# Tile addresses modulo 128 bytes, and weight sums by halves, in a one-core hybrid decoder layer

## The chip, the cores and the metric

The kernel runs on one core of a Trainium2 chip. Its time is the device time of one execution in microseconds (us); the median of several executions is given, and lower is better.

## What is computed

One decoder layer on 256 tokens of width 1024, all in float32. The input is normalised, multiplied by one wide weight matrix, and the product is cut into the operands of three gated branches:

```python
h = rms_norm(x, norm_g)
qa, ka, va, ga, ub, vb, gb, qc, gc, ma, mb, mc = split_cols(h @ w_in, IN_SPLITS)
out_a = moba_attention(rope(qa), rope(ka), va) * silu(ga)          # 6 heads of 128, causal
out_b = gmlp_spatial_gate(ub, vb, ln_g, w_spatial, b_spatial) * silu(gb)   # 6 groups of 128
out_c = memory_cross_attention(qc, rms_norm(mem), w_mem_kv) * silu(gc)     # 4 heads of 128
y = sigmoid(ma) * (out_a @ w_branch_a) + sigmoid(mb) * (out_b @ w_branch_b) + sigmoid(mc) * (out_c @ w_branch_c)
return rms_norm(x + y @ w_out, final_norm_g)
```

With 256 tokens there is one attention block, so the attention is plain causal attention over all tokens. The wide product dominates: w_in alone has 1024 x 9472 floats.

## The kernel before, in words

**Products.** Float32 operands are split into a high part (rounded to the matmul's own format, by ScalarE, ACT) and a low part (the rest, by VectorE, DVE), and a product is made of three matmuls: high by high, high by low, low by high. Activations are split once; weights are split as they arrive, 128 partitions x 1024 floats at a time. Such a piece is called a chunk. split_hi (L258) writes tile hi and split_lo (L262) writes tile lo; each has five slots (SPL = 5), so chunk c uses the slot of chunk c - 5. The splits of chunk c are issued four chunks (LEAD = 4) ahead of its matmuls.

**Kinds of chunks**, in the order that plan() writes out by hand:
- mvk (8) and tok (4): keys and values of the memory, and some columns of v and of the spatial gate (L479, L500, L506).
- fea (30): 128 output columns each, the weights being the stationary operand and the activations n the moving one: eight matmuls of 512 columns and eight of 256 (L628). q, k, ga, gc, qc and parts of ub and gb are made so.
- st (70, in 35 pairs): a Strassen-like scheme. For each of five groups g (two blocks of 512 output columns each), seven blocks i replace eight products; the weights of a block are one of four weight blocks, or sums of them. Order: 1, 2, 5, 3, 6, 7, 4. A pair is one block, its chunks the two halves: six matmuls of 512 columns each (L568), with n or s (sums of n) as stationary operand and hi or lo moving. Group 0 gives columns of va and vb, group 1 ut and gt, groups 2, 3 and 4 the three sigmoid gates (tiles sig and sigs).
- br (16): the three branch projections, with ah and al, obh and obl, och and ocl as stationary operands, twelve matmuls of 512 columns a chunk (L446 to L448, in mm3). Between them stand the last eleven blocks of st.
- out (8): the output projection, with y as stationary operand (L446 to L448 again).

**The form tiles.** The weights of the st blocks live in two tiles of 1 MB, form0 and form1. FORMS says which tile and which weight block a block i uses; the two change places with every group. Blocks 1, 2 and 3 are plain loads, issued on SP's queue (form_load, L226). Blocks 5, 7 and 4 are made by a transfer that adds to what is there, issued on POOL's queue (form_add, L229). Block 6 adds block 3's weights, which the other tile holds at that time: in groups 0, 1 and 2 (SUMS) by a DVE instruction over the whole tile (form_sum, L240), in groups 3 and 4 by an adding transfer. All of these go by whole blocks: a transfer or a sum is issued when both halves of what the tile held have been split. Each is issued at a fixed place in the order of chunks (the lists dma, ready and free at the end of the kernel):

```python
at = free[b] + (chunks[c][2] not in (5, 6, 4, 7))     # a load one chunk later than an addition
if chunks[c][2] == 6 and chunks[c][1] in SUMS:
    at = free[1 - b]
...
free[b] = c + 2 - LEAD
```

**Other weights** come by plain loads on SP's queue into three tiles raw of 1 MB (load, L208), from pair 18 to 46 in two parts.

**Side work** (attention, gates, norms, drains of PSUM) is put between the chunks by a small planner (class Units): each step has an engine, a cost, what it comes after, and a chunk by which it is due. slot() issues what fits before and after each chunk's matmuls. A step that comes after a TensorE step is due four chunks behind that one, so that the PSUM bank comes free.

**Places of the tiles.** Pools lay their tags one behind the other in the order of first use, each as long as its largest tile. Pool act has, in this order: p1, p2, mr, xr, x2 (m, later s), och, ocl, n2 (n, later y), v0 (va, later obl), vb (later obh), trig (the rotary tables, later wspb: spatial weights and their bias, 774 floats a partition), lng, ut, gt, ga (later ah), sg0, sg1, gc (later al0), ub, v1 (al1). Pool wts follows: raw, hi, lo, f0.

Of the kernel before, what the change touches and what calls it, by code (L numbers as in the profile page):

```python
# [24 lines left out]
F32 = mybir.dt.float32  # L25
# [3 lines left out]
OP = mybir.AluOpType  # L29
# [6 lines left out]
HA, GB, HC = 6, 6, 4  # L36
# [4 lines left out]
CH = 1024  # L41
PIECE = 2 * CH
# [3 lines left out]
SPAN = {"fea": 2.78, "st": 1.365}  # L46
# [35 lines left out]
PE, DVE, ACT, POOL, QUEUE = range(5)  # L82


class Units:
# [29 lines left out]

    def fits(self, u, i, pe, now):
        name, e, us, fn, after, wait, due = u
        due = min([due] + [self.pe[a] + 4 for a in after if a in self.pe])
        if pe != (e == PE) or any(a not in self.end for a in after):
            return False  # L120
        if i >= due or e is None:
            return True
        if pe:
            return self.ready(after) + self.margin <= now
        if e == QUEUE:

            return self.ready(after) <= now
        lead = 0.5 if e == POOL else max(0.3, self.room - (2.4 if e == ACT else 1.3) - self.ahead - us)
        return self.t[e] <= now + lead and self.ready(after) <= max(now, self.t[e]) + 0.3

    def slot(self, i, pe):

        now, u = self.t[PE], True
        while u:
            if pe:
                now = self.t[PE]
            u = next((u for u in self.todo if self.fits(u, i, pe, now)), None)
            if u:
                self.todo.remove(u)
                name, e, us, fn, after, wait, due = u  # L140
                if e == PE:
                    self.pe[name] = i
                at = self.ready(after)
                self.end[name] = (at if e is None else self.run(e, us, at)) + wait
                fn()
# [3 lines left out]
def tile_hybrid_layer(ctx: ExitStack, tc: tile.TileContext, mw, xT, mem, x, fin_g, ln_g, w, ws, w_sp, b_sp, rope, out):  # L149
    nc = tc.nc  # L150
# [3 lines left out]
    wts = ctx.enter_context(tc.tile_pool(name="wts", bufs=1))  # L154
# [3 lines left out]
    V = {}  # L158

    def slot_tile(name, shape, tag, dt=F32):  # L160
        V[name] = act.tile(shape, dt, name=name, tag=tag)
        return V[name]
# [17 lines left out]
        return slice(h * 128, (h + 1) * 128)  # L180


    RAW, SPL, LEAD, JT = 3, 5, 4, 2
    raw, hi, lo = {}, {}, {}
    chunks = []
# [23 lines left out]

    def load(j):  # L210
        raw_alloc(j)
        parts = 2 if 18 <= j < 47 else 1
        for i in range(parts):
            load_part(j, i * PIECE // parts, (i + 1) * PIECE // parts)

    def block(g, i):

        return bass.AP(tensor=ws.tensor, offset=ws.offset + (4 * g + i) * 128 * PIECE, ap=[[PIECE, 128], [1, PIECE]])

    def form_tile(i):  # L220
        if f"form{i}" not in V:
            V[f"form{i}"] = (wts if i == 0 else act).tile([128, PIECE], F32, name=f"form{i}", tag=("f0", "mr")[i])
        return V[f"form{i}"]

    def form_load(i, g, b):
        nc.sync.dma_start(form_tile(i), block(g, b))  # L226

    def form_add(i, g, b):
        nc.gpsimd.dma_start(form_tile(i), block(g, b), accum_op=OP.add)  # L229


    SUMS = (0, 1, 2)
    FORMS = {1: (0, 0), 5: (0, 1), 6: (0, 3), 4: (0, 2), 2: (1, 2), 7: (1, 1), 3: (1, 3)}

    def buf(g, i):
        return FORMS[i][0] ^ (g % 2)

    def form_sum(i, g, b):

        nc.vector.tensor_tensor(form_tile(i), form_tile(i), form_tile(1 - i), OP.add)  # L240
        U.run(DVE, 2.35)

    def form_step(g, i):

        if i == 6 and g in SUMS:
            return form_sum, buf(g, i), g, 3

        return (form_add if i in (5, 6, 4, 7) else form_load, buf(g, i), g, FORMS[i][1])

    def split_alloc(c):  # L250
        if "hi" not in V:
            for n in ("hi", "lo"):
                V[n] = wts.tile([128, SPL, CH], F32R, name=n, tag=n)
        hi[c], lo[c] = V["hi"][:, c % SPL, :], V["lo"][:, c % SPL, :]

# [21 lines left out]
    st = [act.tile([128, NG + 4 * XW], F32, name="st0", tag="p1"), act.tile([128, 4 * XW], F32, name="st1", tag="p2")]  # L277
# [164 lines left out]
    U = Units(4.5, AHEAD, 1.8)  # L442
# [251 lines left out]
        nc.sync.dma_start(V["lng"], rows(ln_g, BW))  # L694

    def load_wsp():
        t = slot_tile("wspb", [128, GB * 128 + GB], "trig")
        nc.sync.dma_start(t, w_sp)
        V["wsp"], V["bst"] = t[:, 0:GB * 128].rearrange("p (g t) -> p g t", g=GB), t[:, GB * 128:]

    def cut_wsp():
        for g in range(GB):
# [11 lines left out]
    for t in range(2):  # L714
        U.add(f"xsq{t}", ACT, 1.25, lambda t=t: row_squares(V["xk"][:, t, :], ssx[:, t:t + 1]), after=[f"load_x{t}"],
              due=2 + t)
# [18 lines left out]
    for i in range(KD // 2):  # L735
        U.chain(f"nx{i}", (ACT, 0.62, lambda i=i: norm_hi(i)), (DVE, 0.7, lambda i=i: norm_lo(i)),
                after=[f"nm{2 * i}", f"nm{2 * i + 1}"] + ["s11"] * (i == 3), due=(6, 6, 8, 9)[i])
    U.chain("sum", *[(DVE, 0.69, lambda i=i: sums(i)) for i in range(4)], after=["nx3"], due=[12, 13, 14, 15])
    for i in range(2):
        U.chain(f"sx{i}", (ACT, 1.05, lambda i=i: sums_hi(i)), (DVE, 1.28, lambda i=i: sums_lo(i)), after=["sum"],  # L740
                due=18 - i)
    for t in range(2):
        U.add(f"msq{t}", ACT, 1.25, lambda t=t: row_squares(V[f"mm{t}"], ssm[:, t:t + 1]),
              after=["load_mem"])
# [168 lines left out]
    for h in range(HC):  # L913
# [3 lines left out]
                after=[f"qc{h}", f"mkf{h | 1}", "sqrts"] + back("p", h))  # L917
        U.chain(f"cn{h}", (DVE, 0.2, lambda h=h: softmax_sum("c", h)), (ACT, 0.85, lambda h=h: softmax_norm("c", h)),
                after=[f"cs{h}"])
# [3 lines left out]
    for h in range(HA):  # L923
        if h % 2 == 0:
            r = h // 2
            U.add(f"rin{r}", QUEUE, 1.6, lambda r=r: rope_move(r, False), wait=8.5,
                  after=[f"{n}{i}" for i in (h, h + 1) for n in "qk"] + ["consts"] + ([f"rout{r - 2}"] if r > 1 else []))
# [5 lines left out]
                after=[f"as{h}"])  # L933
        U.chain(f"ap{h}", (PE, 0.33, lambda h=h: a_pT(h)), (ACT, 0.52, lambda h=h: a_pT_out(h)),
                after=[f"an{h}"] + back("v", HC + h))
# [3 lines left out]
    for name, n in (("gc", HC), ("ga", HA)):  # L939
        U.add(name + "s", ACT, n * 0.25, lambda name=name: nc.scalar.activation(V[name], V[name], AF.Silu),  # L940
              after=["exps"] + [f"{name}{i}" for i in range(n)])
    U.add("silu", ACT, 1.4, lambda: nc.scalar.preload_act_table(AF.Sigmoid), after=["gcs", "gas", "gts.0", "gbs2"])

    for t in range(2):
        U.chain(f"lna{t}", (DVE, 1.0, lambda t=t: ln_centre(t)), (ACT, 0.9, lambda t=t: ln_scale(t)), after=["lnr", "gmlp"],
                due=[at_br[0, 0] - 10 + t, at_br[0, 0] - 8 + t])
# [61 lines left out]
    for i in range(3):  # L1008
        hs = slice(2 * i, 2 * i + 2)
        U.add(f"ga_{i}", DVE, 0.69, lambda hs=hs: gate_unit(V["qk"][:, hs, 0, :], V["ga"][:, hs, :]),  # L1010
              after=[f"av{2 * i}", f"av{2 * i + 1}", "gas"], due=at_br[0, 0] - 6)
# [3 lines left out]
          after=[f"cs{h}" for h in range(HC)])  # L1015
    U.chain("gts", (ACT, 1.1, lambda: nc.scalar.activation(V["gt"], V["gt"], AF.Silu)),
            (DVE, 1.25, lambda: nc.vector.tensor_tensor(V["ut"], V["ut"], V["gt"], OP.mult)),
            due=[at_br[0, 0] - 4, at_br[0, 0] - 3], after=["exps", "w11_1", "w12_1", "w22_1", "p14"])
    for i in range(2):
# [6 lines left out]
        after=["mix2", "gbs2"], due=chunks.index(("fea", "gb", 5)) + 5)  # L1026
    U.add("obTa", None, 0, alloc(("obh", [128, GB, S], "vb", F32R), ("obl", [128, GB, S], "v0", F32R)),
          after=["mix0", "mix1", "mix2"])
# [113 lines left out]
        nc.sync.dma_start(out[:, t, 512:D], z[:, 512:D])  # L1142


    dma, ready, free = {}, {}, [6, 9]
    for c in range(n_br):
        if chunks[c][0] == "st" and chunks[c][3] == 0:
            b = buf(*chunks[c][1:3])
            at = free[b] + (chunks[c][2] not in (5, 6, 4, 7))
            if chunks[c][2] == 6 and chunks[c][1] in SUMS:  # L1150
                at = free[1 - b]
            dma.setdefault(at, []).append(form_step(*chunks[c][1:3]))
            ready[c // 2] = at
            free[b] = c + 2 - LEAD
    pace = lambda c: 5.0 + sum(SPAN.get(k[0], 2.73) for k in chunks[:c])
    for c, at in ready.items():
        i = chunks[2 * c][2]
        ready[c] = pace(at) + (2.5 if i == 6 and chunks[2 * c][1] in SUMS else 10.0 if i in (4, 5, 6, 7) else 6.0)
    for c in range(n_br + 4):
        now[0] = c  # L1160
        if c == n_br:
            nc.scalar.preload_act_table(AF.Sqrt)
            residual_parts()
        if c == n_br - 8:
            load_x()
        s = c + (LEAD if c > 9 else 3)
        for fn, *args in dma.pop(c, []):
            fn(*args)
        U.room = sum(SPAN.get(k[0], 2.73) for k in chunks[c:c + LEAD])
        U.slot(c, False)  # L1170
        if c in (7, 8):
            split_lo(2 * c - 6)
            U.end[f"s{2 * c - 6}"] = U.run(DVE, 1.23, U.t[ACT])
        for e in {5: (), 6: (), 7: (9,), 8: (11,), 9: (12, 13)}.get(c, (s,) if s > 3 else ()):
            if chunks[e][0] == "st":
                raw[e // 2] = form_tile(buf(*chunks[e][1:3]))
                came = ready[e // 2]
            else:
                came = {4: 24.0, 5: 25.5}.get(e // 2, 0.0)
            (split_mvk if e < KD else split)(e)  # L1180
            U.end[f"s{e}"] = U.run(DVE, 1.23, U.run(ACT, 1.05, max(U.end.get(f"c{e - SPL}", 0), came)))
        if c in (6, 7):
            split_alloc(2 * c - 4)
            split_hi(2 * c - 4)
            U.run(ACT, 1.05, (23.5, 28.0)[c - 6])
        s += c == 9
        if s % 2 == 1 and s // 2 in PLAIN:
            q = PLAIN.index(s // 2) + 2
            if 4 < q < len(PLAIN):
                load(PLAIN[q])  # L1190
            if q == 6:
                load_mem()
        kind = chunks[c][0]
        U.end[f"c{c}"] = U.run(PE, SPAN.get(kind, 2.73), U.end.get(f"s{c}", 0.0))
        if kind == "mvk":
            mm_mvk(c)
        elif kind == "tok":
            mm_tok(c)
        elif kind == "fea":
            mm_fea(c)  # L1200
        elif kind == "br":
            mm_br(c)
        elif kind == "st":
            mm_st(c)
        else:
            mm_out(c, 0)
            for a, b in (((0, 256), (256, 512)) if chunks[c][1] else ((0, 512),)):
                mm_out(c, 1, a, b)
        U.slot(c, True)
# [115 lines left out]
```

## Time and profile before

| | |
|---|---|
| median of 3 runs | 329.92 us (329.75 to 330.6) |
| the profiled execution: its own time, and its span | 333.19 us, 331.5 us |
| busy: TensorE, DVE, ACT, POOL | 317.0, 255.5, 226.8, 25.0 us |
| mean granted TensorE clock | 0.979 |
| moved by DMA | 77.24 MB, mean 233 GB/s |
| adding transfers into the form tiles (POOL's queue) | 17 of 1 MB, 9.7 us from issue to landing |
| loads into the form tiles (SP's queue) | 15 of 1 MB, 5.0 us |

The span runs from the first to the last instruction. PE is TensorE's matmuls, PEld its loads of the stationary operand. A row of a view names the line of the kernel, the engine, the operation, and the tiles as "written<-read"; acc and aux are PSUM banks. "x" counts instructions, "<-" behind an idle time names what ended it. The granted clock is the share of TensorE's full clock.

### The profile page before, as it was taken

What the parts mean: (1) busy time and instruction counts of PE and PEld (TensorE: products, weight loads), DVE (VectorE), ACT (ScalarE), POOL (GpSimd) and SP (SyncE); (2) the same over time, 40 slices, a digit from 0 to 9 for tenths busy, and PEclk for the clock granted to TensorE, in tenths of its full rate; (3) what the DMA queues carried; (4) which work ended last, traced back from release to release, by engine and by line L of the source; (5) the groups of instructions that cost most, each with busy time, mean ns of one, the idle gap of its engine ahead of it and who ended that gap; (6) DMA issues with size and microseconds to landing.
All of it is one profiled execution on the core that took longest, in us unless ns stands there. A gap on an engine that the chain in (4) does not pass through costs nothing. (4 is left out here: it accounts for less than half of the span.)

```text
span 331.5 us, 4343 instructions
## 1 busy us (share of the span) xinstructions
PE 317.0 (96%) x1542; PEld 261.6 (79%) x1542; DVE 255.5 (77%) x369; ACT 226.8 (68%) x357; POOL 25.0 (8%) x42
## 2 busy tenths in 40 slices
PE   7999999999999999999999999989999897999992
PEld 3888888888888888888888888867887675878882
DVE  2889989977698986975986999846982939889532
ACT  3877979547977869779957967819672744487333
POOL 1000030020010011022011010111010111000022
PEclk9999999999999999999999999997999797999997
DMA  7999998669669489869659789898799697943003
GB/s 205 407 401 417 406 284 288 228 150 190 245 217 259 156 257 213 280 223 222 207 190 173 225 334 211 253 265 165 264 312 292 173 266 133 378 175 128 2 0 127
DMA packets 16294, 77.24 MB, mean 233 GB/s; under 512 B 2064, under 2 KB 3088, under 8 KB 9744
## 3 DMA queue, kind: packets, MB, share of 16 engines
q1 hardware_dynamic: 13680, 59.00, 48.3%
q0 software_dynamic: 2448, 17.83, 28.4%
q8 instruction: 12, 0.20, 0.2%
q10 hardware_dynamic: 144, 0.13, 0.1%
q14 instruction: 10, 0.08, 0.1%
HBM read 75.12 MB, written 1.05 MB: 230 GB/s over the span
## 5 line engine op out<-in xcount | busy, mean ns | idle before, releaser
L262 DVE TENSOR_TENSOR lo<-form,hi 128x1024 fp32r<-128x1024 f32 x70 | 84.1, 1219 | 35.9 <-ACT hi L258 35.5
L258 ACT ACTIVATE hi<-form 128x1024 fp32r<-128x1024 f32 x70 | 72.2, 1056 | 44.8 <-DMA form<-in_ws_dram 33.3
L262 DVE TENSOR_TENSOR lo<-raw,hi 128x1024 fp32r<-128x1024 f32 x58 | 70.0, 1221 | 12.6 <-ACT hi L258 12.2
L258 ACT ACTIVATE hi<-raw 128x1024 fp32r<-128x1024 f32 x58 | 60.8, 1058 | 14.1 <-PE acc L448 4.7
L628 PE MATMUL acc<-n,hi 128*128 128x512 f32 x240 | 61.3, 397 | 0.0
L628 PEld LDWEIGHTS acc<-n,hi 128*128 128x128 f32 x240 | 43.7, 188 | 9.0
L229 POOL DMA_DIRECT2D form<-in_ws_dram x17 | 14.9, 876 | 255.4 <-DVE lo L262 151.0
L568 PE MATMUL acc<-hi,s 128*128 128x512 f32 x96 | 33.1, 403 | 0.0
L628 PEld LDWEIGHTS acc<-n,lo 128*128 128x128 f32 x240 | 30.9, 188 | 1.5
L628 PE MATMUL acc<-n,lo 128*128 128x256 f32 x240 | 31.9, 283 | 0.0
L568 PE MATMUL aux<-hi,s 128*128 128x512 f32 x64 | 24.0, 440 | 2.5 <-ACT hi L258 2.5
L568 PE MATMUL acc<-hi,n 128*128 128x512 f32 x72 | 25.3, 408 | 0.0
L568 PEld LDWEIGHTS acc<-hi,s 128*128 128x128 f32 x96 | 18.0, 188 | 4.2
L568 PE MATMUL acc<-lo,s 128*128 128x512 f32 x48 | 18.9, 394 | 0.0
L568 PEld LDWEIGHTS aux<-hi,s 128*128 128x128 f32 x64 | 13.5, 211 | 6.5 <-ACT hi L258 3.3
L568 PE MATMUL aux<-lo,s 128*128 128x512 f32 x32 | 14.6, 457 | 3.9 <-DVE lo L262 3.9
L568 PE MATMUL aux<-hi,n 128*128 128x512 f32 x48 | 15.9, 395 | 0.0
L568 PEld LDWEIGHTS acc<-hi,n 128*128 128x128 f32 x72 | 13.5, 188 | 3.0
L568 PE MATMUL acc<-lo,n 128*128 128x512 f32 x36 | 14.2, 394 | 0.0
L568 PEld LDWEIGHTS aux<-lo,s 128*128 128x128 f32 x32 | 6.6, 206 | 6.9 <-DVE lo L262 5.5
L568 PEld LDWEIGHTS aux<-hi,n 128*128 128x128 f32 x48 | 9.0, 187 | 2.2
L568 PEld LDWEIGHTS acc<-lo,s 128*128 128x128 f32 x48 | 9.0, 188 | 1.9
(233 smaller groups left out, 578.9 us busy)
## 6 DMA issues: line engine op xcount, KB each, us to landing
raw<-in_w_dram SPq DMA_DIRECT2D x18, 1024.0 KB, 8.7
form<-in_ws_dram POOLq DMA_DIRECT2D x17, 1024.0 KB, 9.7
form<-in_ws_dram SPq DMA_DIRECT2D x15, 1024.0 KB, 5.0
raw<-in_w_dram SPq DMA_DIRECT2D x22, 512.0 KB, 7.2
st<-in_mw_dram SPq DMA_DIRECT2D x7, 384.0 KB, 7.5
raw<-in_w_dram SPq DMA_DIRECT2D x8, 256.0 KB, 7.3
xk<-in_x_dram SPq DMA_DIRECT2D x2, 512.0 KB, 7.5
xt<-in_xT_dram SPq DMA_DIRECT2D x2, 512.0 KB, 8.6
```

Source lines behind the costliest of these rows:

```text
L229: nc.gpsimd.dma_start(form_tile(i), block(g, b), accum_op=OP.add)
L258: nc.scalar.activation(hi[c][:, a:b], raw[c // 2][:, o + a:o + b], AF.Copy)
L262: nc.vector.tensor_tensor(lo[c][:, a:b], raw[c // 2][:, o + a:o + b], hi[c][:, a:b].bitcast(F32), OP.subtract)
L568: nc.tensor.matmul(p, x[:, k0 + k, tsl(t)], wt[c][:, a * 512:(a + 1) * 512], start=first and a + j == 0, stop=half == 1 and a + j == 3, sk ...
L628: nc.tensor.matmul(o, wt, m, start=i == 0, stop=i == len(passes) - 1, skip_group_check=True)
```

## The change

1. The tile wspb is 800 floats wide instead of 774; what is read and written in it stays. A pad LOPAD between hi and lo is added, of size 0.
2. Transfers and sums of the form tiles go by halves: 128 x 1024 floats, 512 KB. Each half has its own place in the order, by its own half's split.
3. Block 6 is a sum on DVE in all five groups.
4. In the planner, a step of ACT that comes after a TensorE step passes on that step's place, so that steps behind it are due four chunks later too; TensorE's own steps no longer take a due place from this.
5. Raw loads go in two parts up to pair 48 instead of 46.

```diff
     def fits(self, u, i, pe, now):
         name, e, us, fn, after, wait, due = u
-        due = min([due] + [self.pe[a] + 4 for a in after if a in self.pe])
+        due = due if pe else min([due] + [int(self.pe[a]) + 4 for a in after if a in self.pe])
...
+                up = [self.pe[a] for a in after if a in self.pe and self.pe[a] % 1 == 0]
                 if e == PE:
                     self.pe[name] = i
+                elif up and e == ACT:
+                    self.pe[name] = up[0] + 0.5
...
+    LOPAD = 0
...
-        parts = 2 if 18 <= j < 47 else 1
+        parts = 2 if 18 <= j < 49 else 1
...
-    def block(g, i):
-        return bass.AP(tensor=ws.tensor, offset=ws.offset + (4 * g + i) * 128 * PIECE, ap=[[PIECE, 128], [1, PIECE]])
+    def block(g, i, h):
+        return bass.AP(tensor=ws.tensor, offset=ws.offset + (4 * g + i) * 128 * PIECE + h * CH, ap=[[PIECE, 128], [1, CH]])
...
-    def form_load(i, g, b):
-        nc.sync.dma_start(form_tile(i), block(g, b))
-    def form_add(i, g, b):
-        nc.gpsimd.dma_start(form_tile(i), block(g, b), accum_op=OP.add)
-    SUMS = (0, 1, 2)
+    def form_half(i, h):
+        return form_tile(i)[:, h * CH:(h + 1) * CH]
+    def form_load(i, g, b, h):
+        nc.sync.dma_start(form_half(i, h), block(g, b, h))
+    def form_add(i, g, b, h):
+        nc.gpsimd.dma_start(form_half(i, h), block(g, b, h), accum_op=OP.add)
+    def form_sum(i, g, b, h):
+        nc.vector.tensor_tensor(form_half(i, h), form_half(i, h), form_half(1 - i, h), OP.add)
+        U.run(DVE, 1.23)
     FORMS = {1: (0, 0), 5: (0, 1), 6: (0, 3), 4: (0, 2), 2: (1, 2), 7: (1, 1), 3: (1, 3)}
...
-    def form_sum(i, g, b):
-        nc.vector.tensor_tensor(form_tile(i), form_tile(i), form_tile(1 - i), OP.add)
-        U.run(DVE, 2.35)
-    def form_step(g, i):
-        if i == 6 and g in SUMS:
-            return form_sum, buf(g, i), g, 3
-        return (form_add if i in (5, 6, 4, 7) else form_load, buf(g, i), g, FORMS[i][1])
+    HOW = {5: (form_add, 8.0), 7: (form_add, 8.0), 4: (form_add, 8.0), 6: (form_sum, 1.5)}
...
-        t = slot_tile("wspb", [128, GB * 128 + GB], "trig")
-        nc.sync.dma_start(t, w_sp)
+        t = slot_tile("wspb", [128, GB * 128 + 32], "trig")
+        nc.sync.dma_start(t[:, 0:GB * 128 + GB], w_sp)
...
-    dma, ready, free = {}, {}, [6, 9]
+    dma, ready, free = {}, {}, [[6, 6], [9, 9]]
+    pace = lambda c: 5.0 + sum(SPAN.get(k[0], 2.73) for k in chunks[:c])
     for c in range(n_br):
-        if chunks[c][0] == "st" and chunks[c][3] == 0:
-            b = buf(*chunks[c][1:3])
-            at = free[b] + (chunks[c][2] not in (5, 6, 4, 7))
-            if chunks[c][2] == 6 and chunks[c][1] in SUMS:
-                at = free[1 - b]
-            dma.setdefault(at, []).append(form_step(*chunks[c][1:3]))
-            ready[c // 2] = at
-            free[b] = c + 2 - LEAD
...
+        if chunks[c][0] == "st":
+            _, g, i, h = chunks[c]
+            b = buf(g, i)
+            fn, us = HOW.get(i, (form_load, 5.0))
+            at = free[1 - b][h] if i == 6 else free[b][h] + (i not in HOW)
+            dma.setdefault(at, []).append((fn, b, g, FORMS[i][1], h))
+            ready[c] = pace(at) + us
+            free[b][h] = c + 1 - LEAD
```

ready[c] is the planner's own estimate of when a piece has landed; it goes into the order of the side work alone.

More of the change, by code (lines that the diff above doesn't have):

```diff
@@ L236, in buf @@
         return FORMS[i][0] ^ (g % 2)
-    def form_sum(i, g, b):
-        nc.vector.tensor_tensor(form_tile(i), form_tile(i), form_tile(1 - i), OP.add)
-        U.run(DVE, 2.35)
-    def form_step(g, i):
-        if i == 6 and g in SUMS:
-            return form_sum, buf(g, i), g, 3
-        return (form_add if i in (5, 6, 4, 7) else form_load, buf(g, i), g, FORMS[i][1])
+    HOW = {5: (form_add, 8.0), 7: (form_add, 8.0), 4: (form_add, 8.0), 6: (form_sum, 1.5)}
     def split_alloc(c):
         if "hi" not in V:
-            for n in ("hi", "lo"):
+            for n, pad in (("hi", 0), ("lo", LOPAD)):
+                if pad:
+                    wts.tile([128, pad], F32, name=n + "pad", tag=n + "pad")
                 V[n] = wts.tile([128, SPL, CH], F32R, name=n, tag=n)
@@ L696, in load_wsp @@
     def load_wsp():
-        t = slot_tile("wspb", [128, GB * 128 + GB], "trig")
-        nc.sync.dma_start(t, w_sp)
-        V["wsp"], V["bst"] = t[:, 0:GB * 128].rearrange("p (g t) -> p g t", g=GB), t[:, GB * 128:]
+        t = slot_tile("wspb", [128, GB * 128 + 32], "trig")
+        nc.sync.dma_start(t[:, 0:GB * 128 + GB], w_sp)
+        V["wsp"], V["bst"] = t[:, 0:GB * 128].rearrange("p (g t) -> p g t", g=GB), t[:, GB * 128:GB * 128 + GB]
     def cut_wsp():
@@ L1142, in out_store @@
         nc.sync.dma_start(out[:, t, 512:D], z[:, 512:D])
-    dma, ready, free = {}, {}, [6, 9]
+    dma, ready, free = {}, {}, [[6, 6], [9, 9]]
+    pace = lambda c: 5.0 + sum(SPAN.get(k[0], 2.73) for k in chunks[:c])
     for c in range(n_br):
-        if chunks[c][0] == "st" and chunks[c][3] == 0:
-            b = buf(*chunks[c][1:3])
-            at = free[b] + (chunks[c][2] not in (5, 6, 4, 7))
-            if chunks[c][2] == 6 and chunks[c][1] in SUMS:
-                at = free[1 - b]
-            dma.setdefault(at, []).append(form_step(*chunks[c][1:3]))
-            ready[c // 2] = at
-            free[b] = c + 2 - LEAD
[L1155 to L1158, printed above, removed]
+        if chunks[c][0] == "st":
[6 more added lines that the diff above has]
+            free[b][h] = c + 1 - LEAD
     for c in range(n_br + 4):
@@ L1176, in tile_hybrid_layer @@
                 raw[e // 2] = form_tile(buf(*chunks[e][1:3]))
-                came = ready[e // 2]
+                came = ready[e]
             else:
```

## The prediction

> **What bounds the kernel now.** I read the page first, for the busy shares and the clock. "q1" is the queue of SP's transfers, "q0" that of POOL's adding ones.
>
> ```profile
> span 331.5 us, 4343 instructions
> PE 317.0 (96%) x1542; PEld 261.6 (79%) x1542; DVE 255.5 (77%) x369; ACT 226.8 (68%) x357; POOL 25.0 (8%) x42
> ...
> PEclk9999999999999999999999999997999797999997
> ...
> q1 hardware_dynamic: 13680, 59.00, 48.3%
> q0 software_dynamic: 2448, 17.83, 28.4%
> ```
>
> TensorE is busy for 96% of the span, so only two things shorten this kernel: matmuls that follow each other faster, and the few places where PE stands or runs at a lower clock. The clock row shows such places in slices 27 to 33 (8.3 us each). The table by stretches sizes them.
>
> ```profile
> 220.00:240.00 20.00, 17.72 (x70) 13.74 (x69) 14.02 (x14) 15.10 (x17) 0.86 (x1) 0.91 0.83 218
> 240.00:260.00 20.00, 18.31 (x77) 14.28 (x76) 11.85 (x13) 11.69 (x14) 0.86 (x1) 0.99 0.95 302
> 260.00:280.00 20.00, 17.57 (x62) 13.34 (x61) 14.11 (x15) 10.18 (x12) 2.60 (x3) 0.84 0.81 174
> ```
>
> Columns: length, busy PE, PEld, DVE, ACT, POOL, granted clock, DMA share, GB/s. PE stands for 2.28 + 1.69 + 2.43 = 6.4 us, and the clock takes 1.8 + 0.2 + 3.2 = 5.2 us more (20 us times what is missing to 1.00): 11.6 us in this stage. The waits from 220 to 280 us and ACT's rows say what ends them.
>
> ```profile
> POOL form L229 <- DVE lo L262: 53.5, 5, 17.2
> ACT hi L258 <- DMA form<-in_ws_dram: 24.5, 5, 7.8
> DVE lo L262 <- ACT hi L258: 21.3, 7, 6.1
> ...
> PE aux L568 <- DVE lo L262: 3.9, 4, 2.1
> PE aux L568 <- ACT hi L258: 2.5, 2, 1.5
> ```
>
> ```profile
> 222.16 2.01 ACT L258 ACTIVATE hi<-form 128x1024 fp32r<-128x1024 f32 x2 [7.77 <-DMA form<-in_ws_dram]
> ...
> 256.44 2.00 ACT L258 ACTIVATE hi<-form 128x1024 fp32r<-128x1024 f32 x2 [5.95 <-DMA form<-in_ws_dram]
> ...
> 269.76 2.01 ACT L258 ACTIVATE hi<-form 128x1024 fp32r<-128x1024 f32 x2 [5.94 <-DMA form<-in_ws_dram]
> ```
>
> Read upwards: PE waits for a split, DVE's half of it for ACT's, and ACT for an adding transfer into a form tile. By order of chunks the three are block 6 of group 3, block 5 of group 4 and block 6 of group 4. Before this stage PE is never without work; there only the rate of the matmuls counts:
>
> ```profile
> 40.00:220.00 180.00, 180.00 (x938) 152.90 (x937) 150.72 (x226) 135.14 (x228) 15.59 (x24) 1.00 0.81 232
> ```
>
> **The rate of the matmuls.** Here the trace has an experiment of its own. These stretches hold 24 matmuls of 512 columns each: two branch chunks with ah and al as stationary operand, two with obh and obl, and four of the Strassen chunks.
>
> ```profile
> 237.02:242.47 5.45, 5.45 (x25) 4.50 (x24) 5.12 (x7) 2.01 (x2) 0.00 (x0) 1.00 0.98 406
> 248.07:253.67 5.60, 5.60 (x25) 4.50 (x24) 2.36 (x2) 2.42 (x4) 0.00 (x0) 1.00 1.02 233
> 207.72:213.32 5.60, 5.60 (x26) 4.50 (x24) 5.21 (x7) 5.60 (x9) 0.86 (x1) 1.00 0.86 281
> ```
>
> 5.45/24 = 227 ns against 5.60/24 = 233 ns, at the same clock; neither DVE's nor the DMA engines' load goes with it (406 GB/s in the faster one). What goes with it is the place of the tiles. Between x2 (m, s), n2 (n, y), v0, vb, och, ocl and the tiles behind "trig" (ga/ah, gc/al0, v1/al1, hi, lo), all sizes are multiples of 128 bytes but one: wspb has 774 floats, 3096 = 24 x 128 + 24. So ah, al, hi and lo begin at one byte modulo 128, and n, s, y, obh and och at another. With 800 floats, 3200 = 25 x 128, all of these agree.
>
> **The change, part by part.**
> 1. *Alignment.* Pairs that now differ: 420 matmuls at L568 (70 half chunks by 6), 240 at L628, 120 of the branches (16 chunks by 12, less ah's 72) and 72 with y: 852 of 512 columns, by 6.2 ns: 5.3 us. Of 256 columns 240 at L628 and 48 with y; no pair of that width is aligned in this trace, so I take half, 3.1 ns, between 0 and 6.2: 0.9 us. Sum **6.2 us**. The chunks before 40 us gain nothing in my sum: the DMA share is 0.96 there, in the table by stretches.
>
> ```profile
> 0.00:40.00 40.00, 37.76 (x173) 29.38 (x174) 30.95 (x57) 29.43 (x51) 1.09 (x9) 1.00 0.96 365
> ```
>
> Bounds: whether a pair is fast because it agrees, or because both begin at a multiple of 128, the trace can't show directly, as after the change the common byte is hi's present one plus the 96 (or 104) bytes that the longer wspb pushes it. If the second, the gain is nothing, ah's 72 lose 0.4 us, and if each operand off its place costs its own 6.2 ns, 6.2 us are lost. For agreement speaks this pair of rows: the Strassen chunks have the shifted tile as stationary operand, the feature chunks as the moving one, and both take the same.
>
> ```profile
> L568 PE MATMUL acc<-hi,n x72: 389/396/587, 45.4 to 198.2; 128*128 128x512 f32 x72
> ...
> L628 PE MATMUL acc<-n,hi x240: 392/395/578, 39.8 to 207.5; 128*128 128x512 f32 x120
> ...
> L447 PE MATMUL acc<-lo,ah x24: 387/389/397, 213.6 to 242.0; 128*128 128x512 f32 x24
> ```
>
> (ns min/median/max of one.) [...] So I take 6.2, nearest to the row of ah.
>
> 2. *Block 6 by DVE in groups 3 and 4 too.* Two adding transfers of 1 MB go. The sum needs only block 3, which landed for the chunk before. The rows of the sums and of the splits:
>
> ```profile
> L240 DVE TENSOR_TENSOR form<-form,form 128x2048 f32<-128x2048 f32 x3 | 6.9, 2285 | 0.0
> L262 DVE TENSOR_TENSOR lo<-form,hi 128x1024 fp32r<-128x1024 f32 x70 | 84.1, 1219 | 35.9 <-ACT hi L258 35.5
> ```
>
> A half costs what a split does: 10 x 1.22 instead of 3 x 2.29 = +5.3 us on DVE, of it 4.9 in the late stage. There the waits at 222 and 270 us lose their cause. Cover: DVE has 65.5 us of work from 209 to 298.
>
> ```profile
> 209.00:298.00 89.00, 82.60 (x331) 64.75 (x330) 65.49 (x72) 52.76 (x59) 6.05 (x7) 0.94 0.85 241
> ```
>
> 65.5 + 4.9 = 70.4 us, while PE would need 89 - 11.6 - 1.6 (alignment) = 75.8: DVE fits at 93%. What is queued behind a sum on DVE is the next chunk's lo, 1.22 us later than without it.
>
> 3. *Halves.* Each half's transfer starts when its own half is split, instead of after both, and is half as long.
>
> ```profile
> raw<-in_w_dram SPq DMA_DIRECT2D x18, 1024.0 KB, 8.7
> form<-in_ws_dram POOLq DMA_DIRECT2D x17, 1024.0 KB, 9.7
> ...
> raw<-in_w_dram SPq DMA_DIRECT2D x22, 512.0 KB, 7.2
> ```
>
> ```profile
> 240.11 1.23 DVE L262 TENSOR_TENSOR lo<-form,hi 128x1024 fp32r<-128x1024 f32 x1 [0.34 <-ACT hi L258]
> ...
> 242.45 1.21 DVE L262 TENSOR_TENSOR lo<-form,hi 128x1024 fp32r<-128x1024 f32 x1
> ```
>
> ```profile
> 244.02 0.86 POOL L229 DMA_DIRECT2D form<-in_ws_dram  x1 [17.18 <-DVE lo L262]
> ```
>
> For block 5 of group 4 the first half may start at 241.3 (240.11 + 1.23) instead of 244.0. A half lands after 4.9 us (half of 9.7) to 9.7 us (size saves nothing); I take 7.2, the row of 512 KB. The whole came at 256.44, 12.4 us after its issue; with halves I put the first near 249 to 251 and the second near 253. PE came to that chunk behind the first of these rows, at 256.5:
>
> ```profile
> 256.24 0.39 PE L568 MATMUL aux<-hi,n 128*128 128x512 f32 x1
> 257.55 0.50 PE L568 MATMUL aux<-hi,s 128*128 128x512 f32 x1 [0.93 <-ACT hi L258]
> ```
>
> So this wait goes too, by some 3 us; at 9.7 from both issues it goes but for the second half's tail. Added issues: 15 on SP and 13 x 0.86 us on POOL, whose queues wait in this stage (53.5 us above); POOL holds nothing else then, and SP's loads wait for the same splits as before. Of 17.83 MB added by transfers, 2 MB go.
>
> Of the 11.6 us I count **10.0**: the rest for waits that come up in its place, as DVE has little left. Bounds 0 to 11.6.
>
> 4. *The order of side work.* DVE steps behind an ACT step that drains a PSUM bank are now due four chunks after the matmul: ga, gc and the obT halves, 0.7 us each, move up. Nothing is added; an early one can hold the next lo by 0.7 us once or twice, or free it later: 0, bounds +-1.4. One more raw load goes in two parts (0.4 us of SP). The pad LOPAD is 0 and does nothing.
>
> **Sum.** 333.19 us is the profiled execution's own time (span 331.5 and 1.7 around it), 1% over the median of the runs, 329.92. 333.2 - 6.2 - 10.0 = 317.0, by 329.92/333.19: **313.9 us**.
>
> [...]
>
> **Rivals.**
> A. *Alignment does nothing.* For it: no pair at the new common byte is in the trace. Against: the equal rows of L568 and L628. 333.2 - 10.0 = 323.2, that is 320.0; with 6.2 lost instead, 326.2.
> B. *The late stage keeps its loss.* DVE at 93%, in order, with sums ahead of the splits, becomes what PE waits for, and the clock drops again. For it: DVE's share; against: ACT's 24.5 us of waits go, which held DVE for 21.3. 333.2 - 6.2 = 327.0, that is 323.8.
> C. *Slower: an adding packet costs by the packet, not by its bytes.* q0's 28.4% are 94 us of all engines for 17 transfers, 615 ns a packet against 187 in q1. If halves cost as much each, 30 take 166 us, 72 more; with 0.83 of the first 302 us used (251 us), that is 323 us of transfers ahead of the output stage's 29.5: 352, that is 349. It makes the kernel slower from 302 - 157 = 145 us for q0 (157 is the rest), 0.87 of a whole one's cost for a half. Against: q1's packets have 0.6 of q0's bytes and 0.3 of its time.
>
> ```profile
> 0.00:302.00 302.00, 293.37 (x1412) 241.44 (x1413) 241.23 (x345) 215.33 (x333) 21.01 (x38) 0.98 0.83 252
> 302.00:331.50 29.50, 23.66 (x131) 20.12 (x129) 14.24 (x25) 11.50 (x25) 4.00 (x4) 0.94 0.12 43
> ```
>
> **How the numbers follow.** The forecast has 0.6, A 0.15, B 0.16, C 0.04, and a mishap that just cancels the gain 0.05. The forecast's own range is 309 (both parts in full: 7.0 with the first chunks, and 11.6, with a little of part 4) to 318. The range for 8 in 10 takes in A and B: 308 to 324.5. Within 0.3% (1 us) is about what a measurement of this kernel can't tell from no change. Faster: forecast, A and B, 0.91; same 0.04; slower 0.05.
>
> **What would show it.** Part 1: 24 matmuls of a Strassen or obh stretch in 5.45 us, and the median of one at 389; at 396 rival A. Part 2: no wait of PE at blocks 6, L240's successor 10 times at 1.22 us, and a clock row without the dips at 27 to 33. Part 3: adds of 512 KB landing near 7 us, and the 24.5 us of ACT's waits down to a few. Wrong if PE's waits are back behind DVE (B), if adds take 9 us each (C), or if a new wait shows between 40 and 220 us, where faster matmuls have less cover.

## The result, and the profile after

The changed kernel takes 320.72 us (median of 4 runs, 319.87 to 321.17) against 329.84 us (329.46 to 330.60) for the kernel before on the same chip: a ratio of 0.9718, 95% interval 0.9690 to 0.9746, or 9.1 us less. The profiled execution of the changed kernel took 320.98 us.

These are the lines of its page that answer to those shown of before: the span, the busy times, the clock row, the two queues, the splits on DVE and ACT, DVE's sums, and the issues (count, KB each, us to landing).

```profile
span 319.2 us, 4440 instructions
PE 312.0 (98%) x1542; PEld 260.1 (81%) x1542; DVE 260.2 (81%) x376; ACT 227.8 (71%) x357; POOL 36.5 (11%) x55
...
PEclk9999999999999999999999999999999999999998
...
q1 hardware_dynamic: 15984, 59.00, 52.3%
q0 software_dynamic: 4320, 15.73, 26.8%
...
L264 DVE TENSOR_TENSOR lo<-form,hi 128x1024 fp32r<-128x1024 f32 x70 | 84.8, 1222 | 16.2 <-ACT hi L260 15.7
L260 ACT ACTIVATE hi<-form 128x1024 fp32r<-128x1024 f32 x70 | 73.4, 1057 | 23.3 <-DMA form<-in_ws_dram 8.6
...
L240 DVE TENSOR_TENSOR form<-form,form 128x1024 f32<-128x1024 f32 x10 | 12.2, 1222 | 0.0
...
form<-in_ws_dram POOLq DMA_DIRECT2D x30, 512.0 KB, 8.5
raw<-in_w_dram SPq DMA_DIRECT2D x24, 512.0 KB, 7.3
```

The dips of the clock at slices 27 to 33 are gone, ACT waits 8.6 us for form tiles where it waited 24.5 in the late stage alone, and PE is busy for 98% of the span. Stretch by stretch (columns as before), with one stretch of four Strassen chunks and one of two branch chunks with obh and obl, 24 matmuls each:

```profile
40.00:220.00 180.00, 180.00 (x938) 153.31 (x937) 156.11 (x234) 141.41 (x235) 24.48 (x35) 1.00 0.84 232
220.00:240.00 20.00, 20.00 (x88) 16.35 (x87) 17.88 (x19) 13.72 (x16) 3.47 (x4) 1.00 1.02 268
240.00:260.00 20.00, 20.00 (x87) 16.21 (x87) 13.71 (x13) 12.94 (x15) 0.86 (x1) 1.00 0.83 266
260.00:280.00 20.00, 19.66 (x85) 15.61 (x84) 19.07 (x22) 12.42 (x13) 2.59 (x3) 1.00 0.97 264
```

```profile
207.61:213.18 5.57, 5.57 (x25) 4.52 (x24) 4.96 (x7) 4.93 (x6) 0.00 (x0) 1.00 0.72 249
243.54:249.11 5.57, 5.57 (x26) 4.52 (x24) 3.58 (x3) 3.37 (x5) 0.00 (x0) 1.00 0.97 268
```

Two readings. The late stage has lost its waits: PE stands for 0.34 us there, not 6.4, and the clock takes nothing. But the matmuls hardly got faster: 5.57/24 = 232 ns, against 233 before and the 227 that was forecast (the median of one at L570 is 393, between the 389 and the 396 that the prediction named as signs). And between 40 and 220 us there are 938 matmuls in both traces. The four-chunk stretch begins at 207.72 us in the trace before and at 207.61 here. The whole gain lies behind it.

### The profile page after: what moved, and what is told of

Read it like the earlier page. It is cut to its first block, busy times and chain, and to the rows that moved or that the text cites. A ratio compares the mean times of both kernels' runs of the same rounds, so it can differ in the third digit from the quotient of the medians.

```text
span 319.2 us, 4440 instructions
## 1 busy us (share of the span) xinstructions
PE 312.0 (98%) x1542; PEld 260.1 (81%) x1542; DVE 260.2 (81%) x376; ACT 227.8 (71%) x357; POOL 36.5 (11%) x55
## 3 DMA queue, kind: packets, MB, share of 16 engines
q0 software_dynamic: 4320, 15.73, 26.8%
## 4 chain that ended last, share of the span: by engine, by line
PE 77%; DMA 9%; DVE 6%; issue 4%; ACT 1%; POOL 0%; SPq 0%; ACTq 0%; POOLq 0%; DVEq 0%
PE acc L630 26%; PE acc L570 18%; DMA form<-in_ws_dram 7%; PE aux L502 3%; PE acc L508 3%; PE aux L570 3%; DVE lo L264 3%; PE acc L450 3%; PE acc L448 3%; PE acc L449 3%; PE aux L781 2%; DMA st<-in_mw_dram 2%; PE aux L481 2%; PE acc L481 2%; DVE form L240 1%
## 5 line engine op out<-in xcount | busy, mean ns | idle before, releaser
L264 DVE TENSOR_TENSOR lo<-form,hi 128x1024 fp32r<-128x1024 f32 x70 | 84.8, 1222 | 16.2 <-ACT hi L260 15.7
L260 ACT ACTIVATE hi<-form 128x1024 fp32r<-128x1024 f32 x70 | 73.4, 1057 | 23.3 <-DMA form<-in_ws_dram 8.6
L236 POOL DMA_DIRECT2D form<-in_ws_dram x30 | 26.1, 871 | 232.9 <-DVE lo L264 84.6
L570 PE MATMUL acc<-hi,s 128*128 128x512 f32 x96 | 33.1, 402 | 0.0
L570 PE MATMUL acc<-hi,n 128*128 128x512 f32 x72 | 25.1, 404 | 0.0
L570 PEld LDWEIGHTS acc<-hi,s 128*128 128x128 f32 x96 | 18.1, 188 | 4.0
L570 PE MATMUL aux<-hi,s 128*128 128x512 f32 x64 | 21.1, 395 | 0.0
L570 PE MATMUL acc<-lo,s 128*128 128x512 f32 x48 | 18.9, 395 | 0.0
L570 PE MATMUL aux<-hi,n 128*128 128x512 f32 x48 | 16.1, 396 | 0.0
L570 PEld LDWEIGHTS acc<-hi,n 128*128 128x128 f32 x72 | 13.6, 188 | 2.9
L570 PEld LDWEIGHTS aux<-hi,s 128*128 128x128 f32 x64 | 12.1, 188 | 2.8
L570 PE MATMUL acc<-lo,n 128*128 128x512 f32 x36 | 14.2, 394 | 0.0
L570 PE MATMUL aux<-lo,s 128*128 128x512 f32 x32 | 12.7, 398 | 0.3 <-DVE lo L264 0.3
L643 ACT ACTIVATE qk<-acc 128x256 f32<-128x256 f32 x12 | 4.7, 390 | 11.7 <-PE acc L630 11.7
L240 DVE TENSOR_TENSOR form<-form,form 128x1024 f32<-128x1024 f32 x10 | 12.2, 1222 | 0.0
L570 PEld LDWEIGHTS aux<-hi,n 128*128 128x128 f32 x48 | 9.0, 188 | 2.1
```

The costliest lines, as they stand in the source:

```text
L236: nc.gpsimd.dma_start(form_half(i, h), block(g, b, h), accum_op=OP.add)
L240: nc.vector.tensor_tensor(form_half(i, h), form_half(i, h), form_half(1 - i, h), OP.add)
L260: nc.scalar.activation(hi[c][:, a:b], raw[c // 2][:, o + a:o + b], AF.Copy)
L264: nc.vector.tensor_tensor(lo[c][:, a:b], raw[c // 2][:, o + a:o + b], hi[c][:, a:b].bitcast(F32), OP.subtract)
L570: nc.tensor.matmul(p, x[:, k0 + k, tsl(t)], wt[c][:, a * 512:(a + 1) * 512], start=first and a + j == 0, stop=half == 1 and a + j == 3, sk ...
```

## The experiments

In each comparison the ratio is to the kernel before, run on the same chip. Two questions were open: why the matmuls kept their rate, and which part gave the 9.1 us.

### What the rate of the matmuls goes by

wspb's length decides where hi, lo, ah and al begin against n, s, y, obh and och. It is 3096 bytes before, and 3200 = 12.5 x 256 in the changed kernel. In the kernel before, hi, lo, ah and al begin at byte 128 modulo 256, the others at 96. The longer tile brings the four to 224: they agree with the rest modulo 128, and miss them by 128 modulo 256. ah and hi agree with each other in any case. So the fast pair (hi, ah) of the trace before could mean modulo 256 or 512 (theories M256 and M512), or a matter of the region of the memory in which ah and al lie (theory R).

**Agreement modulo 512.** `[128, GB * 128 + 32]` becomes `[128, 896]` (3584 = 7 x 512 bytes).

> The changed kernel with wspb 896 floats wide instead of 800, so that hi, lo, ah and al move by 384 bytes more and every tile read by TensorE (m, s, n, y, och, obh, ah, hi, lo) begins at byte 96 modulo 512. In the changed kernel hi, lo and ah begin at 224 modulo 512 and the others at 96, and only the pairs with ah run at 227 ns, the others at 232. Theory M (agreement counts, but modulo 256 or 512 bytes and not 128): stretches of 24 matmuls in 5.45 us instead of 5.57, 852 x 5 ns = 4.3 us, and 256-column matmuls from 119 to about 114 ns, 288 x 5 = 1.4 us: 315 to 316.5 us. Theory R (what counts is that both operands lie in the upper part of SBUF, as with ah): no change, 320.7 us within 1 us, matmul medians 393 and 389 as before.

Measured: 317.93 us (6 runs), ratio 0.9635 (0.9587 to 0.9683). Behind the first 40 us the 512-column matmuls follow each other at 226 to 227 ns (medians, from one start to the next) in every pair of tiles. The rate is theory M's; its time, 315 to 316.5 us, is missed, as it had put 1.4 us on 256-column matmuls that did not speed up.

**Agreement modulo 256 only.** The same line with `[128, 832]` (3328 = 13 x 256 bytes).

> The same with wspb 832 floats wide: hi, lo, ah and al at byte 352 modulo 512, the others at 96, so that they agree modulo 256 and not modulo 512. Theory M with modulus 256: as the run with 896 floats, 315 to 316.5 us. Theory M with modulus 512: ah's pairs alone at 389 ns, the others at 393 to 396, 320.7 us within 1. Theory R: the same as that, 320.7 us.

Measured: 317.17 us (4 runs), ratio 0.9620 (0.9580 to 0.9661). The same two stretches, and the line of the Strassen chunks, in this variant:

```profile
205.37:210.81 5.44, 5.44 (x25) 4.50 (x24) 5.44 (x8) 4.93 (x6) 0.00 (x0) 1.00 0.75 264
240.73:246.17 5.44, 5.44 (x25) 4.50 (x24) 3.59 (x3) 3.45 (x5) 0.00 (x0) 1.00 1.02 331
```

```profile
L570 PE MATMUL acc<-hi,n x72: 387/389/590, 44.9 to 196.0; 128*128 128x512 f32 x72
```

5.44/24 = 227 ns: the fast rate, with agreement modulo 256 and not modulo 512. M512 and R fall. It is also the fastest kernel of the study, 3.5 us under the changed one. The 852 matmuls of 512 columns at 5 ns would make 4.3 us. The 256-column ones give a little of it back (119 ns became 120 here; 117 in the kernel before).

**lo alone moved by 128 bytes.** In the changed kernel `LOPAD = 0` becomes `LOPAD = 32`: lo now agrees with n, s and obh modulo 256 and no longer with ah, hi stays.

> The changed kernel with LOPAD at 32 floats, which moves lo alone by 128 bytes. Theory M: the pairs of lo with ah lose their agreement, and the median of acc<-lo,ah goes from 389 to 393 ns or more while hi's pairs may stay; time within 1 us of 320.7. Theory R: ah's three rows stay at 389 ns.

Measured: 322.17 us (one run). The rates part within one execution; the branch chunks' matmuls (ns min/median/max of one):

```profile
L448 PE MATMUL acc<-hi,ah x24: 397/397/398, 212.7 to 237.0; 128*128 128x512 f32 x24
L449 PE MATMUL acc<-lo,ah x24: 395/395/395, 212.9 to 237.3; 128*128 128x512 f32 x24
L449 PE MATMUL acc<-lo,obh x24: 388/388/396, 243.5 to 273.3; 128*128 128x512 f32 x24
```

Of one tile, lo, the pair with obh is now the fast one and that with ah the slow one, where the changed kernel has it the other way round (392 and 389). So it is not the tile alone that sets the rate. Nor is it the pair alone: hi and ah begin at the same byte modulo 256 as before, yet their matmuls, each followed by one of lo with ah, went from 389 to 397, which is 236 ns from one start to the next. The time, 1.5 us over the changed kernel's, is more than the 1 us that was expected, on a single run.

**No alignment at all.** The changed kernel with wspb at its old 774 floats.

> The changed kernel with the alignment alone undone: wspb 774 floats wide again, all else as changed (halves, block 6 on VectorE in all groups, planner). The forecast's step 1 (6.2 us from alignment) expects 326 to 327 us. The reading of the two traces (512-column matmuls from 234 to 232 ns, 256-column ones from 117 to 119) expects 320.7 to 321.7 us.

Measured: 320.58 us (6 runs), ratio 0.9732 (0.9698 to 0.9765), against 320.72 with it. Agreement modulo 128 is worth nothing.

**Agreement modulo 256 alone, on the kernel before.** wspb of 832 floats, nothing else changed.

> The kernel before with wspb of 832 floats alone: the stationary and moving tiles agree modulo 256, all else as before. Theory U (rate of the matmuls is independent of the rest): 512-column matmuls at 227 ns in place of 233, and the 3.5 us that the same edit gave the changed kernel: 326 to 327. Theory L (what PE gains it loses again standing for the same transfers in the late stage, which come no sooner): 328.5 to 330, with the median of L568 at 389 all the same.

Measured: 326.23 us (6 runs), ratio 0.9892 (0.9854 to 0.9929): 3.6 us less, what it gave the changed kernel. Theory U holds in its time, L in one stage. Against the second execution of the kernel before (below), PE is 3.1 us ahead at the four-chunk stretch (204.92 against 208.00) and 3.2 us at the last branch chunk (291.31 against 294.48): what the first 208 us gain is kept, and what the matmuls of the late stage gain goes into its waits, which are still there (PE stands for 6.8 us from 215 to 285 us, against 5.8 in that execution).

**lo off by 32 bytes.** The variant with 832 floats and `LOPAD = 8`.

> The variant whose tiles agree modulo 256 (317.17), with lo alone moved by 32 bytes: hi, ah, al and n, s, y, och, obh still agree, lo differs from them by 32. Asked: do the 256-column matmuls (n stationary, lo moving; 117 ns where the two differ by 32 or 96 bytes modulo 128, 119 to 120 where they agree or differ by 128) follow the agreement modulo 128, against the rest? If yes (theory C): 117 for n,lo and 232 to 234 for the 512-column pairs with lo as stationary operand (about 256 of them), 227 still for those with hi. 240 x 3 ns gained against 256 x 6 lost: 317.5 to 318.5. If not (theory O, lo's own pair does not set it): 120 and the same losses: 318.5 to 319.5.

(In the kernel lo is the moving operand of the 512-column matmuls and the stationary one of those with 256; the expectation names them the other way round.)

Measured: 319.45 us (4 runs), ratio 0.9698 (0.9634 to 0.9763), within theory O's time, though neither theory named the rates whole. lo's 512-column pairs go at 234 to 237 ns (medians of one 394 to 399), slower than the 232 to 234 of both. n,lo with 256 columns goes at 118 (281, against 283 with agreement), between the two. And most of hi's pairs, which still agree, slowed from 227 to between 230 and 232 (with n and s from 389 to 392 and 393; with obl and ocl to 226 to 228). As with hi and ah in the run with lo moved by 128 bytes, pairs that agree took longer between pairs that do not. Why is not shown, and it is not always so: in that run lo and obh, which agree, kept 388 ns between matmuls of hi and obh at 393. What the 256-column matmuls go by, and what in the chip makes agreement fast, stays open.

### Which part removed the waits

**Block 6 of groups 3 and 4 by adding transfers again.** In the changed kernel:

```
- fn, us = HOW.get(i, (form_load, 5.0))
- at = free[1 - b][h] if i == 6 else free[b][h] + (i not in HOW)
+ fn, us = (form_add, 8.0) if i == 6 and g > 2 else HOW.get(i, (form_load, 5.0))
+ at = free[1 - b][h] if fn is form_sum else free[b][h] + (i not in HOW)
```

> The changed kernel (alignment to 128 as in the change) with block 6 of groups 3 and 4 made by adding transfers of 512 KB again; groups 0 to 2 keep VectorE's sums. Theory S (VectorE's sums are what took the waits of the late stage away): ACT waits at the blocks 6 of groups 3 and 4 again, PE behind it, the clock drops there: 325 to 328 us. Theory H (the halves alone do it, as an adding half that starts with its own half's split lands in time): no such waits, VectorE has 4.9 us less to do: 320 to 321.5 us.

Measured: 323.52 us (6 runs), ratio 0.9822 (0.9784 to 0.9861), 2.8 us more than the changed kernel. Neither theory holds whole: the waits at the blocks 6 are back, as S had it, but the granted clock stays at 1.00 from 220 to 280 us. PE loses 1.0 us at 223.0 and 1.0 us at 266.1 (from one start to the next, less the 0.23 of a matmul), behind these splits, the chunks of block 6:

```profile
221.92 1.06 ACT L260 ACTIVATE hi<-form 128x1024 fp32r<-128x1024 f32 x1 [0.60 <-DMA form<-in_ws_dram]
```

```profile
265.03 1.06 ACT L260 ACTIVATE hi<-form 128x1024 fp32r<-128x1024 f32 x1 [3.02 <-DMA form<-in_ws_dram]
```

**The sums alone.** The kernel before with `SUMS = (0, 1, 2, 3, 4)`.

> The kernel before with VectorE's whole-block sums for block 6 in all five groups (SUMS with 3 and 4 too), nothing else of the change: 1 MB transfers, alignment as before. Theory S: the waits at 222 and 270 us go, the one at 256 us (block 5 of group 4) stays with its drop of the clock: 323 to 326 us. Theory H: the adding blocks come as late as before, little gained: 328 to 330 us.

Measured: 328.39 us (8 runs), ratio 0.9953 (0.9925 to 0.9981). The time is theory H's, the waits are theory S's: PE stands 0.3 us at 222 us and not at all at 270, and the wait for block 5 of group 4 remains. ACT waits 7.86 us for it, PE stands for 2.8 us, and the clock (0.92 and 0.91 in the stretches from 240 to 280 us) takes 3.4 us more:

```profile
256.03 2.00 ACT L258 ACTIVATE hi<-form 128x1024 fp32r<-128x1024 f32 x2 [7.86 <-DMA form<-in_ws_dram]
```

**The old order of side work.** The changed kernel without the two edits of the planner. (The program comes out the same if only the second, which marks ACT's drains, is undone.)

```
- due = due if pe else min([due] + [int(self.pe[a]) + 4 for a in after if a in self.pe])
+ due = min([due] + [self.pe[a] + 4 for a in after if a in self.pe])
...
- elif up and e == ACT:
-     self.pe[name] = up[0] + 0.5
```

> The changed kernel with the two edits of the planner undone (due times of steps behind a draining ACT step). Part 4 of the forecast put them at 0 with bounds of 1.4 us: 320.7 us within 1.4. A rival: the earlier gates of branch a are what gives VectorE its place in the late stage; then the wait at block 6 of group 4 (0.5 us in the changed kernel) grows and 322 to 324 us are measured.

Measured: 327.88 us (6 runs), ratio 0.9926 (0.9907 to 0.9945): 7.2 us more than the changed kernel, far outside anything that the prediction gave this step. PE's timeline, the table of its waits, the stretch with its clock, and DVE's and ACT's timelines show where:

```profile
210.28 0.40 PE L568 MATMUL aux<-hi,n 128*128 128x512 f32 x1
214.42 0.71 PE L568 MATMUL aux<-hi,s 128*128 128x512 f32 x1 [3.74 <-DVE sigs L582]
```

```profile
PE aux L568 <- DVE sigs L582: 3.7, 1, 3.7
```

```profile
200.00:220.00 20.00, 16.26 (x77) 13.30 (x76) 16.55 (x21) 13.45 (x21) 0.86 (x1) 0.91 0.69 206
```

```profile
200.17 0.69 DVE L981 TENSOR_TENSOR mid<-mid,gc 128x512 f32<-128x512 f32 x1
...
208.64 1.22 DVE L262 TENSOR_TENSOR lo<-form,hi 128x1024 fp32r<-128x1024 f32 x1 [2.39 <-ACT hi L258]
...
213.59 0.69 DVE L582 TENSOR_TENSOR sigs<-aux,sigs 128x512 f32<-128x512 f32 x1
```

```profile
204.51 1.66 ACT L986 ACTIVATE ah<-qk 128x512 fp32r<-128x512 f32 x3
206.07 1.07 ACT L986 ACTIVATE obh<-aux 128x512 fp32r<-128x512 f32 x2
207.03 0.64 ACT L986 ACTIVATE och<-mid 128x512 fp32r<-128x512 f32 x1
207.55 1.06 ACT L258 ACTIVATE hi<-form 128x1024 fp32r<-128x1024 f32 x1
```

The gated branch outputs (mid) are ready at 200.9, so that ACT splits ah, obh and och in one block of 3.2 us ahead of a hi. DVE waits 2.39 us for that hi, its sigs comes at 213.59, and PE waits 3.74 us for the PSUM bank that sigs empties; then the clock is 0.5 for 3.4 us, 1.7 us more (0.91 in the stretch). Two later waits behind DVE's lo make another 1.1 us. In the changed kernel the same pair of mid runs at 191.00, and ACT's splits fall into time in which it has nothing else:

```profile
191.00 1.29 DVE L983 TENSOR_TENSOR mid<-mid,gc 128x512 f32<-128x512 f32 x2
```

```profile
192.26 1.66 ACT L988 ACTIVATE ah<-qk 128x512 fp32r<-128x512 f32 x3
```

**The planner's edits alone,** on the kernel before.

> The kernel before with only the planner's two edits (due times of DVE steps behind an ACT step); sums, whole blocks and addresses as before. Theory W: the edit is worth its 7 us (327.88 against 320.7) wherever it stands: about 323, and the drains of the gates come 10 us sooner. Theory J: the edit counts only where halves and sums have brought PE close behind DVE; here PE stands for transfers (block 6 of group 3, block 5 of group 4) and these waits stay: 328.5 to 330.5, ratio 0.996 to 1.002.

Measured: 330.49 us (12 runs), ratio 1.0032 (1.0003 to 1.0061). Theory J holds; W falls: by itself the edit gains nothing.

**The planner's edits and the sums,** on the kernel before: all of the change but the halves, what comes with them (the planner's estimates of landing, and two raw loads in two parts) and the addresses.

> The kernel before with the planner's two edits and block 6 summed by DVE in all groups, blocks still whole; only halves (and addresses, worth nothing) are lacking to the changed kernel's 320.7; without the planner's edits it was 328.39. Theory H (halves are needed for block 5 of group 4): the wait of 3 us there and 1 to 2 us behind it stay: 324.5 to 328.5. Theory P (the planner's order and the sums are all, halves give nothing): 320 to 322.

Measured: 328.88 us (12 runs), ratio 0.9969 (0.9944 to 0.9995), just above theory H's range. PE stands for 5.6 us from 220 to 280 us. At block 5 of group 4 it is 1.4 us, behind ACT, which waits for the whole transfer. The rest is at the blocks 6: 2.4 us before 227 and 1.8 at 272. There ACT waits for DVE's sums of whole blocks (form<-form, L243), and side work between the two halves' splits (ACT's in group 3, DVE's in group 4) adds to it:

```profile
220.76 1.06 ACT L261 ACTIVATE hi<-form 128x1024 fp32r<-128x1024 f32 x1 [6.01 <-DVE form L243]
...
255.04 2.00 ACT L261 ACTIVATE hi<-form 128x1024 fp32r<-128x1024 f32 x2 [5.62 <-DMA form<-in_ws_dram]
...
265.93 2.01 ACT L261 ACTIVATE hi<-form 128x1024 fp32r<-128x1024 f32 x2 [4.61 <-DVE form L243]
```

PE's waits of the whole run, by what ended them:

```profile
PE aux L571 <- DVE lo L265: 4.1, 4, 1.8
PE aux L571 <- ACT hi L261: 1.5, 3, 0.6
```

With block 6 summed in all groups this makes a table of four (us; alignment modulo 128 left out, as it is worth nothing):

| | old order | new order |
|---|---|---|
| whole blocks | 328.39 | 328.88 |
| halves | 327.88 | 320.58 |

Each of the two, halves (with what comes with them) and order, is worth under 1 us without the other, and 7.3 to 8.3 us with it. Halves take away the waits for transfers and, with the new order, those for sums of whole blocks; with the old order they also shift eight transposes (L779, aux<-ident,ut) into the middle of a feature chunk, from 200.98 us in the kernel with sums alone to 204.03, and a later chunk then meets the bank that sigs still holds. In the kernel with sums alone sigs comes as late, at 213.23, and PE does not wait for it. That the shift is what makes PE wait was read from the timelines; no run changes it alone.

**The kernel before once more.**

> The kernel before itself, for a second profile: the first one's own time was 333.19 us against a median of 329.9. If the 3.3 us lie in the late stage, PE's standing and the clock take 8 to 9 us from 220 to 280 us here instead of 11.6, and the profiled execution takes about 330 us; if they lie elsewhere, the stage shows 11 to 12 us again.

Its profiled execution took 328.55 us, span 326.8, against the 333.19 of the first one:

```profile
220.00:240.00 20.00, 18.59 (x79) 14.38 (x78) 15.86 (x17) 16.18 (x17) 0.86 (x1) 1.00 0.89 233
240.00:260.00 20.00, 19.23 (x83) 15.15 (x82) 13.03 (x14) 13.40 (x15) 1.73 (x2) 1.00 0.94 276
260.00:280.00 20.00, 16.35 (x69) 12.35 (x68) 14.19 (x15) 8.41 (x9) 1.74 (x2) 1.00 0.90 204
```

PE stands for 5.8 us here, much as in the first (6.4), but the clock stays at 1.00: the 5.2 us that the clock took are not in every execution. How usual they are can be read from the mean granted clock of each run: 0.979 in the first profile, 0.994 in this one, a median of 0.990 over 53 other runs of the kernel before, and 0.995 to 0.998 in the four of the changed kernel. Times the span, what is missing to 1.00 makes 6.9, 2.0, 3.3 and 0.6 to 1.6 us, the output stage included. By this estimate the first profile lost 3.6 us more than a usual run, about the 3.3 us by which it lay above the median, and some 2 of the 9.1 us gained are the clock's.

## Why the prediction was right, and where it was not

The forecast was 313.9 us; it came to 320.72, on the predicted side and within the range, 6.8 us above the likeliest value. Between the two profiled executions it made 16.2 us and found 333.19 - 320.98 = 12.2: 6.2 less at step 1, 2.2 more elsewhere. The remaining 2.8 us are the scaling of the terms to the median, which took 3.1 us off where 0.3 were due.

*Step 1, alignment (6.2 us) failed.* The trace's own pair, 5.45 against 5.60 us, was real, and so was the reading that it goes by the places of the two tiles against each other and not by one tile's own start (though with lo moved the matmuls of hi and ah went from 389 to 397 ns at unchanged places). The modulus was wrong. hi, lo and ah agree modulo 256 in the kernel before, and the step took the first modulus that the change's own sizes offered, though 3200 bytes are 12.5 x 256. What it should have asked is by how much the fast pair agrees. Measured: nothing (320.58 us without, 320.72 with). Modulo 256 it is 3.5 us, not 6.2, since 256-column matmuls lose 2 to 3 ns each where the step gave them 3.1 ns of gain (288 x 3 = 0.9 us lost and 0.9 not gained), and 512-column ones settle at 227 from the 232 that they had at the new place. Rival A, alignment that does nothing, is what happened. That its 320.0 us comes within 0.7 of the measured time is in part luck: the 2.8 us of the scaling and the 2.2 us that were found elsewhere nearly cancel.

*Steps 2 and 3 were right in mechanism.* The waits named, at block 6 of group 3, block 5 of group 4 and block 6 of group 4, went. One thing the prediction didn't see: with the new order the blocks 6 need the halves as well, as with sums of whole blocks PE stands for 4.2 us there (2.4 and 1.8, in the run with order and sums). DVE's added work was forecast as 5.3 us and is 260.2 - 255.5 = 4.7. A half sum takes 1222 ns against 1.22 us forecast. Block 5 of group 4 comes by its halves, issued at 235.68 and 238.10 us; its splits are the first two of these rows:

```profile
245.86 1.05 ACT L260 ACTIVATE hi<-form 128x1024 fp32r<-128x1024 f32 x1
250.49 1.06 ACT L260 ACTIVATE hi<-form 128x1024 fp32r<-128x1024 f32 x1 [3.58 <-DMA form<-in_ws_dram]
251.45 1.99 ACT L260 ACTIVATE hi<-raw 128x1024 fp32r<-128x1024 f32 x2
```

The second half was put at 253 and is split from 250.49 on; PE comes to it at 253.3. One size was off: a half lands after 8.5 us (median), not 7.2, nearer to the whole block's 9.7 than the middle that was taken, and this second half was split only 12.4 us after its issue. Against whole blocks of 9.2 and 9.0 us in two other traces a half saves 0.5 to 0.7. The slack bore it: hi is there 1.75 us before PE needs it. Only 0.34 us of waiting is left, where DVE has four drains of branch b ahead of a lo.

What was mis-sized is the step's sum. 11.3 of 11.6 us went in the profiled execution, more than the 10.0 forecast. But 5.2 of these were the clock's, and a usual run of the kernel before has only part of them, the second profile none. Multiplying by 329.92/333.19 took 1% off the forecast's whole time, where the excess of the one execution lay mostly in this term.

*Step 4, the order (0, bounds +-1.4), was mis-sized.* Alone it measures +0.6 us (330.49 against 329.86), as forecast. With the halves it is worth 7.3. The step was costed against the order of the kernel before, but the planner makes its order anew for every change of a cost or due time, and the order with halves has a wait of 3.74 us that the kernel before does not have. So the halves' own step lacked the same amount as a cost: without this edit the kernel ends at 327.9. That the sum of steps 2 and 3 came out is therefore partly luck: it rests on an edit that the prediction put at 0.

*Rival B* (the late stage keeps its loss) did not come: the clock row has no dip, and DVE, at 17.88, 13.71 and 19.07 of 20 us in the three stretches, keeps up. *Rival C* (adding packets cost by the packet) is refuted: 26.8% of 16 x 319.2 us over 4320 packets are 317 ns each against 615 for packets of twice the size. Here the cost goes by bytes. From issue to landing, 30 adds of 512 KB take 8.5 us each (median) against 9.0 for the whole blocks of the kernel with sums and order, so one of them is the worse bargain by its bytes, and yet with halves the kernel ends 8.3 us sooner: the first half, of a transfer as of a sum, can start before the second is free.

## What to carry to other kernels

When a trace holds a fast and a slow instance of one instruction, work out every modulus by which their addresses agree before you trust the one that the change is about; here padding to a multiple of 128 bytes gave nothing (320.72 us against 320.58 without), and to a multiple of 256 it gave 3.5 and 3.6 us on the two versions of the kernel. A planner's order is part of every edit that feeds it: two edits that are worth under 1 us alone were worth over 7 us together, so price an order against the program as changed, not against the one before. Look at a second execution before you count a clock dip as a term: here the waits came again (5.8 us against 6.4), the dips did not (a clock of 1.00 in all three stretches, against 0.91, 0.99 and 0.84).

## What was not expected of the hardware

- In these traces the rate of 512-column matmuls goes by the addresses of their operands: 227 ns where all stationary and moving tiles agree modulo 256 bytes, 231 to 235 ns where the two miss throughout, by 32 or by 128 (medians of one 389 against 392 to 397). Matmuls of 256 columns go the other way, 120 against 117 ns (agreeing, and missing by 32; medians of one 283 against 280).
- Some pairs that agree took longer between pairs that do not: with lo alone off by 32 bytes most of hi's pairs went at 230 to 232 ns, and with lo off from ah by 128 hi and ah, which agree, went at 236. In the latter run lo and obh, which agree too, stayed at 388 ns (median of one) between matmuls of 393.
- Behind five stands of PE (2.3, 1.7 and 2.4 us in the first trace of the kernel before, 2.8 with the sums alone, 3.7 with the old order; in one piece or in two within 5 us) the granted clock fell to 0.5 for 3.4 us (6.9 us once). In the second execution of the kernel before it stayed at 1.00 through the same waits, 2.1 us at 270 us among them.
